# A hybrid decoder step on one core: the paged past's keys and values fetched and multiplied in alternating slots

## The chip, the cores and the metric

The program runs on 1 core of one Trainium2 chip. The engines named are PE (TensorE), DVE (VectorE), ACT (ScalarE), POOL (GpSimd, whose queue issues the page fetches) and SP (whose queue issues the other transfers). The metric is device time in microseconds of one execution; 3 runs of the kernel before are given, and one profiled execution whose trace is read.

## The reference

Two layers. Each has a half-step SwiGLU, a mixer (an SSD scan beside stick-breaking attention, one input and one output projection) and a second SwiGLU. A prompt of 16 + 512 tokens and 8 samples of 8 tokens go through together. What the change touches is the samples' attention to a past of 2048 keys, kept in pages:

```python
def sb_block(q, start, k, v, key_valid, bias):
    z = jnp.einsum('bqhd,bkhd->bhqk', q, k).astype(jnp.float32) * (SB_HEAD_DIM ** -0.5)
    z = z + bias.astype(jnp.float32)[None, :, None, None]
    ...
    log_stay = jnp.where(allowed, jax.nn.log_sigmoid(-z), 0.0)
    log_after = lax.cumsum(log_stay, axis=3, reverse=True) - log_stay
    w = jnp.where(allowed, jnp.exp(jax.nn.log_sigmoid(z) + log_after), 0.0)
    return jnp.einsum('bhqk,bkhd->bqhd', w.astype(v.dtype), v)
...
        k_past = cache_k[l][page_table].reshape(db, -1, SB_HEADS, SB_HEAD_DIM)
        v_past = cache_v[l][page_table].reshape(db, -1, SB_HEADS, SB_HEAD_DIM)
        xs, c_s, s_s, k_s, v_s = layer(xs, lp, state_conv[l], state_ssm[l], k_past, v_past, 0)
```

A weight of a key depends on all later keys of its sample (the reversed cumulative sum), so no value can be weighed before all scores of its sample are there.

## The kernel before

All 592 tokens stand as columns, 128 features to a tile. Projections and feed-forward layers are `gemm`: for each output tile, 128x296 matmuls into PSUM tiles `g`, three for each weight tile (high and low parts of both sides), by `mm3` (L605). Weights come as `raw` tiles and are split into `whi` on ACT (L595) and `wlo` on DVE (L596).

A mixer spills the residual stream, projects queries and values (`values`, L926), and then the rest of its steps are written in the order of `ORDER` (convolution, `k`, `z`, the scan in six chunks, prompt attention in 12 units, and so on), with the paged past written ahead of them all. The order in which they run is another one: a scheduler takes instructions by priority, which is the place in the program unless `ahead` moves it. `UNIT` and `PRI` hold such places, counted from the start of the past: `"ps0": 507` means that the scores of sample 0 are taken as if they stood 507 instructions behind that start. Each engine then runs its own list in that order and stops at an instruction whose inputs aren't there. So all of this is one interleaving, and `together` adds one rule: matmuls of a group stand in a row, and the first of them takes over the waits of all.

The past of a layer, in `past`: for each sample 8 key pages and 8 value pages (here a "page" is one indirect fetch of 128x1024 float32, 512 KB, on POOL's queue, L1487 and L1552). `past_scores` goes through four quarters: fetch two key pages into `kn` buffers, transpose them on DVE into two `kt` tiles (L1493), 16 matmuls into `sc`; after every second quarter sigmoids on ACT write `pbe` and `pst` (four buffers). `past_weights` makes the running product on DVE (L1298), carries it across partitions by two small transposes on PE (of `tot`, L1518, and of `car`, L1524), multiplies (L1530), transposes eight tiles (L1534) and copies them to `wt` (L1536). `past_values` goes through four quarters of two value pages, each 8 matmuls into `po`, and ends with `ob` (L1565) and two small matmuls (L1569). Key and value pages share six buffers of tag `kn`; `kt` has two, `sc` and `po` one each. The program writes the scores of sample s, then the values of sample s-1, then the weights of sample s.

The first half of the output projection `w_out` (192 matmuls of `g` from `mh`/`ml`, L605 again) needs only the scan's side. Its four parts are tied behind the last scores, weights and values; the second half needs everything, and starts behind it.

Of the kernel before, what the change touches and what calls it, by code (L numbers as in the profile page):

```python
# [8 lines left out]
F32 = mybir.dt.float32  # L9
# [75 lines left out]
def pack(d):  # L85
# [21 lines left out]
class Kern:  # L107
# [1350 lines left out]
    def past(self):  # L1458
        self.oP = self.cp.tile([128, 4, 64], F32, name="oP", tag="oP")
        todo = None  # L1460
        for s in range(8):
            with self.ahead("ps", s):
                be, st = self.past_scores(s)
            if todo:
                with self.ahead("pv", s - 1):
                    self.past_values(*todo)
            with self.ahead("pw", s):
                todo = (s, *self.past_weights(s, be, st))
        with self.ahead("pv", 7):
            self.past_values(*todo)  # L1470

    def past_scores(self, s):
        nc, l = self.nc, self.l
        qbd = self.QBD[0]
        for a in range(4):
            nc.scalar.copy(qbd[32 * a:32 * a + 32, :, a, :].rearrange("p (b m) q -> p b m q", b=4),
                                  self.rep[32 * a:32 * a + 32, :, :, 8 * s:8 * s + 8])
        be = [self.kv.tile([128, 512], F32, name="pbe", tag="pb", bufs=4) for _ in range(2)]
        st = [self.kv.tile([128, 512], F32, name="pst", tag="pb", bufs=4) for _ in range(2)]
        for half in range(2):  # L1480
            sc = self.own("sc", [128, 2, 256])
            for tb in range(2):
                kns, kts = [], []
                for u in range(2):
                    kn = self.kv.tile([128, 1024], F32, name="kn", tag="kn", bufs=6)
                    i = 4 * half + 2 * tb + u
                    nc.gpsimd.indirect_dma_start(kn, None, self.kflat,  # L1487
                                                 bass.IndirectOffsetOnAxis(ap=self.kidx[l][:, s, i:i + 1], axis=0))
                    kns.append(kn.rearrange("p (t c) -> p t c", t=2))
                for quad in range(2):  # L1490
                    kt = self.kv.tile([128, 4, 8, 32], F32, name="kt", tag="kt")
                    for u in range(2):
                        nc.vector.transpose(kt[:, 2 * u:2 * u + 2].rearrange("p t h i -> p t (h i)"),  # L1493
                                            kns[u][:, :, 256 * quad:256 * quad + 256])
                    kts.append(kt)
                with self.together():
                    for quad, dh, i in ((quad, dh, i) for quad in range(2) for dh in range(2) for i in range(4)):
                        h = 4 * quad + i
                        hd = 4 * (2 * (h % 2) + dh) + h // 2
                        self.last_sc = self.mm(sc[32 * i:32 * i + 32, quad, 128 * tb:128 * tb + 128],  # L1500
                                qbd[:, hd].rearrange("p a q -> p (a q)"), kts[quad][:, :, 2 * i + dh, :],
                                start=(dh == 0), stop=(dh == 1))
            for quad in range(2):
                c = 2 * l + quad
                f = lambda t: t.rearrange("p (i t) -> p i t", t=16)[:, :, 8 * half:8 * half + 8]
                self.sigmoids(f(be[quad]), f(st[quad]), sc[:, quad].rearrange("p (t i) -> p i t", t=8),
                              self.bq[:, c:c + 1], self.bq[:, 4 + c:5 + c])
        return be, st

    def past_weights(self, s, be, st):  # L1510
        nc = self.nc
# [15 lines left out]
        wts = []  # L1527
# [11 lines left out]
        return wts,  # L1539

    def past_values(self, s, wts):

        nc, l = self.nc, self.l
        po = self.own("po", [128, 512])
        for e in range(2):
            for a2 in range(2):
                vs = []
                for a in (2 * a2, 2 * a2 + 1):
                    tag, bufs = ("kt", 2) if s == 7 and e + a2 == 2 else ("kn", 6)
                    v = self.kv.tile([128, 2, 512], F32, name="v", tag=tag, bufs=bufs)  # L1550
                    i = s * 4 + a
                    nc.gpsimd.indirect_dma_start(v.rearrange("p k c -> p (k c)"), None, self.vflat,  # L1552
                                                 bass.IndirectOffsetOnAxis(ap=self.vidx[l][:, i, e:e + 1], axis=0))
                    vs.append((a, v))
                with self.together():
                    for a, v in vs:
                        for j in range(2):
                            for quad in range(2):
# [64 lines left out]
```

## Time and profile before

| what | value |
|---|---|
| median of 3 runs | 2719.44 us (2717.28 to 2721.03) |
| profiled execution | 2716.29 us |
| its span, first to last instruction | 2714.5 us |
| granted TensorE clock, mean | 0.983 |
| PE, DVE, ACT, POOL busy | 96%, 55%, 36%, 12% of the span |
| `g` matmuls on PE (L605) | 53% of the chain that ended last |
| key pages, value pages fetched | 128 and 128, 134 MB |

Busy times count an engine as busy while any instruction of it is in flight; matmuls overlap, so that a busy PE may still have room. A wait is put down to the semaphore that came last. A stretch is given in us from the span's start; layer 0's mixer lies between about 509 and 930 us, layer 1's between about 1854 and 2280.

### The profile page before, as it was taken

How to read it: one execution, taken by the hardware profiler on the slowest of the kernel's cores; microseconds unless marked ns; L12 is line 12 of the kernel's file. 1: busy time of each engine (PE TensorE's matmuls, PEld its weight loads, DVE VectorE, ACT ScalarE, POOL GpSimd, SP SyncE). 2: the span in 40 equal slices, each digit the busy share in tenths (PEclk: the TensorE clock that was granted, in tenths of full speed). 3: DMA queues.
4: the chain of work that ended last, by engine and by line, in shares of the span. 5: the costliest groups of instructions: out<-in, count | busy, mean ns of one | idle time of the engine just before them, and what ended most of it. 6: DMA issues, size and time to landing. Idle time of an engine off the chain costs nothing.

```text
span 2714.5 us, 51301 instructions
## 1 busy us (share of the span) xinstructions
PE 2611.9 (96%) x21547; PEld 2469.2 (91%) x21547; DVE 1505.0 (55%) x3005; ACT 981.8 (36%) x1773; POOL 315.6 (12%) x288
## 2 busy tenths in 40 slices
PE   8999999999878999999999999999997899999999
PEld 7999999888656999999999999998875579999999
DVE  5444345477886744444554343454777867434444
ACT  3323224255654332222332222233556544323222
POOL 1000000024443100000000000000334431000000
PEclk9999999999998999999999999999998989999999
DMA  3232234347776122222222323254577762222222
GB/s 111 79 116 86 79 109 130 125 142 262 269 267 230 55 78 86 86 78 78 78 78 79 101 85 94 74 157 125 183 248 247 256 219 71 78 86 86 78 87 81
DMA packets 245111, 343.28 MB, mean 126 GB/s; under 512 B 32808, under 2 KB 196720, under 8 KB 244880
## 3 DMA queue, kind: packets, MB, share of 16 engines
q1 hardware_dynamic: 208016, 205.77, 24.5%
q0 software_dynamic: 36864, 134.23, 14.5%
q8 instruction: 169, 2.77, 0.4%
q14 instruction: 62, 0.51, 0.1%
HBM read 320.29 MB, written 19.66 MB: 125 GB/s over the span
## 4 chain that ended last, share of the span: by engine, by line
PE 60%; DVE 6%; DMA 3%; ACT 2%; issue 1%; POOL 0%; SPq 0%; DVEq 0%; ACTq 0%; POOLq 0%
PE g L605 53%; DVE kt L1493 2%; DMA v<-in_cache_v,vi 1%; PE v L926 1%; DMA kn<-in_cache_k,ki 1%; PE po L208 1%; PE po L211 1%; DVE st L1298 1%; DVE x L799 0%; PE pw L476 0%; PE z L211 0%; PE sc L211 0%; DVE pst L1298 0%; PE zt L1350 0%; PE pw L1534 0%
## 5 line engine op out<-in xcount | busy, mean ns | idle before, releaser
L605 PE MATMUL g<-xl,whi 128*128 128x296 f32 (+1 forms) x3392 | 1016.9, 300 | 1.7 <-DVE xl L447 1.7
L605 PE MATMUL g<-xh,wlo 128*128 128x296 f32 (+1 forms) x3392 | 1012.5, 299 | 3.4 <-DVE wlo L596 3.4
L605 PE MATMUL g<-xh,whi 128*128 128x296 f32 (+1 forms) x3392 | 1013.8, 300 | 1.6 <-DVE gs L231 1.2
L595 ACT ACTIVATE whi<-raw 128x512 fp32r<-128x512 f32 (+1 forms) x664 | 412.7, 622 | 1363.5 <-PE g L605 1280.4
L596 DVE TENSOR_TENSOR wlo<-raw,whi 128x512 fp32r<-128x512 f32 (+1 forms) x664 | 450.7, 679 | 598.0 <-ACT whi L595 541.1
L605 PEld LDWEIGHTS g<-xh,wlo 128*128 128x128 f32 x3392 | 640.2, 189 | 5.4 <-DVE wlo L596 4.1
L605 PEld LDWEIGHTS g<-xh,whi 128*128 128x128 f32 x3392 | 639.6, 189 | 6.0 <-issue 2.6
L605 PEld LDWEIGHTS g<-xl,whi 128*128 128x128 f32 x3392 | 640.6, 189 | 4.8 <-DVE xl L447 2.8
L605 PE MATMUL g<-hl,whi 128*128 128x296 f32 (+1 forms) x1408 | 417.9, 297 | 0.0
L605 PE MATMUL g<-hh,wlo 128*128 128x296 f32 (+1 forms) x1408 | 417.7, 298 | 0.0
L605 PE MATMUL g<-hh,whi 128*128 128x296 f32 (+1 forms) x1408 | 416.8, 298 | 0.0
L1487 POOL DMA_INDIRECT kn<-in_cache_k,ki x128 | 137.0, 1070 | 1554.6 <-PE g L605 931.5
L605 PEld LDWEIGHTS g<-hl,whi 128*128 128x128 f32 x1408 | 265.2, 188 | 0.0
L605 PEld LDWEIGHTS g<-hh,wlo 128*128 128x128 f32 x1408 | 264.3, 188 | 0.0
L605 PEld LDWEIGHTS g<-hh,whi 128*128 128x128 f32 x1408 | 263.9, 188 | 0.0
L1493 DVE STREAM_TRANSPOSE kt<-kn 128x512 f32<-128x512 f32 x256 | 163.4, 680 | 41.8 <-PE sc L211 21.7
L1552 POOL DMA_INDIRECT v<-in_cache_v,vi x128 | 144.2, 1127 | 280.6 <-DVE kt L1493 128.0
L704 DVE SCALAR_TENSOR_TENSOR x<-g,x 128x296 f32<-128x296 f32 (+1 forms) x192 | 88.2, 464 | 119.1 <-PE g L605 118.5
L231 DVE TENSOR_TENSOR us<-g,R 128x296 f32<-128x296 f32 (+1 forms) x176 | 81.6, 464 | 129.5 <-PE g L605 129.4
L231 DVE TENSOR_TENSOR gs<-g,R 128x296 f32<-128x296 f32 (+1 forms) x176 | 80.7, 464 | 123.1 <-PE g L605 121.4
L691 ACT ACTIVATE hh<-us 128x592 fp32r<-128x592 f32 (+1 forms) x88 | 61.2, 696 | 62.4 <-DVE us L689 62.4
L605 PE MATMUL g<-mh,whi 128*128 128x296 f32 (+1 forms) x256 | 78.0, 305 | 2.0 <-DVE ot L231 2.0
(372 smaller groups left out, 2894.5 us busy)
## 6 DMA issues: line engine op xcount, KB each, us to landing
raw<-in_ffn_w_gu SPq DMA_DIRECT2D x176, 512.0 KB
raw<-in_ffn_w_down SPq DMA_DIRECT2D x80, 512.0 KB
raw<-in_w_in SPq DMA_DIRECT2D x44, 512.0 KB
raw<-in_w_out SPq DMA_DIRECT2D x16, 512.0 KB
spill<-x SPq DMA_DIRECT2D x16, 296.0 KB
x<-spill SPq DMA_DIRECT2D x16, 296.0 KB
raw<-in_ffn_w_down SPq DMA_DIRECT2D x16, 256.0 KB
xt<-in_x_prompt SPq DMA_DIRECT2D x8, 256.0 KB
```

What stands on the lines that cost most here:

```text
L208: i = self.nc.tensor.matmul(*a, **k).ins
L211: i = self.nc.tensor.matmul(*a, **k).ins
L231: self.nc.vector.tensor_tensor(tv[0:P, h, :], ps[h][0:P, 0:self.n], rv[0:P, h, :], ALU.mult)
L595: nc.scalar.activation(hi[:, 0:nk], s, AF.Copy)
L596: nc.vector.tensor_tensor(lo[:, 0:nk], s, hi[:, 0:nk].bitcast(F32), ALU.subtract)
L605: mm = nc.tensor.matmul(ps[h][:, 0:self.n], w[:, k, :], self.hv(x)[:, h, :], start=(first and k == 0 and i == 0), stop=(last and k == nk - ...
L691: nc.scalar.activation(hh[:, a:b], u[:, a:b], AF.Copy)
L704: nc.vector.scalar_tensor_tensor(v, p, 0.5, v, ALU.mult, ALU.add)
L926: nc.tensor.matmul(ps[c], x[:, t0:t0 + 128], w.rearrange("p x c -> p (x c)"), start=(k == 0 and i == 0), stop=(k == 7 and i == 2))
L1487: nc.gpsimd.indirect_dma_start(kn, None, self.kflat, bass.IndirectOffsetOnAxis(ap=self.kidx[l][:, s, i:i + 1], axis=0))
L1493: nc.vector.transpose(kt[:, 2 * u:2 * u + 2].rearrange("p t h i -> p t (h i)"), kns[u][:, :, 256 * quad:256 * quad + 256])
L1552: nc.gpsimd.indirect_dma_start(v.rearrange("p k c -> p (k c)"), None, self.vflat, bass.IndirectOffsetOnAxis(ap=self.vidx[l][:, i, e:e + 1] ...
```

## The change

The past is written as 34 slots and four value quarters behind them. Slot x fetches the two key pages of quarter x (four quarters to a sample) and, from slot 6, the two value pages of quarter x - 6; transposes the keys; and multiplies scores and values in one `together` group. A sample's weights are made at the end of its fourth slot, so that its values begin two slots later (slot 4s + 6). In the last two slots there are values alone, and the last sample's four value quarters follow. Operations, shapes, tags and numbers of buffers are what they were; the functions are cut anew. The 13 entries of `UNIT` for the past's units are dropped, so that the past stands at its own place in the program, ahead of all that follows; the other entries stay.

```diff
--- before.py
+++ after.py
@@ -97,8 +97,8 @@
 UNIT = {
     "conv0": 296, "conv2": 988, "conv3": 1825, "conv5": 1898, "k1": 434, "k2": 1127, "k3": 936, "prompt0": 1013,
     "prompt1": 2161, "prompt11": 2222, "prompt2": 2280, "prompt3": 1185, "prompt4": 2319, "prompt5": 1429,
-    "prompt6": 106, "prompt7": 1403, "ps0": 507, "ps3": 2030, "ps4": 1648, "ps7": 1031, "pv0": 0, "pv3": 1421,
-    "pv7": 1019, "pw0": 408, "pw3": 532, "pw4": 1425, "pw5": 0, "pw6": 2149, "pw7": 619, "scan0": 467, "scan2": 75,
+    "prompt6": 106, "prompt7": 1403,
+    "scan0": 467, "scan2": 75,
     "scan3": 879, "scan5": 123, "wo0": 0, "wo1": 2358, "wo2": 1775, "wo3": 86, "wo4": 1087, "wo5": 1599, "wo6": 529,
     "wo7": 1477, "z1": 0, "z2": 970, "z3": 1087,
 }
@@ -1456,56 +1456,78 @@
         nc.scalar.activation(self.on, po, AF.Copy)
 
     def past(self):
+
+
+        nc, l = self.nc, self.l
         self.oP = self.cp.tile([128, 4, 64], F32, name="oP", tag="oP")
-        todo = None
-        for s in range(8):
-            with self.ahead("ps", s):
-                be, st = self.past_scores(s)
-            if todo:
-                with self.ahead("pv", s - 1):
-                    self.past_values(*todo)
-            with self.ahead("pw", s):
-                todo = (s, *self.past_weights(s, be, st))
-        with self.ahead("pv", 7):
-            self.past_values(*todo)
-
...
+        wts = {}
+        late = lambda x: (x // 4, x % 4)
+        for x in range(34):
+            s, i = late(x)
+            v, vi = late(x - 6)
+            if s < 8 and i == 0:
+                qbd = self.QBD[0]
+                for a in range(4):
+                    nc.scalar.copy(qbd[32 * a:32 * a + 32, :, a, :].rearrange("p (b m) q -> p b m q", b=4),
+                                   self.rep[32 * a:32 * a + 32, :, :, 8 * s:8 * s + 8])
+                be = [self.kv.tile([128, 512], F32, name="pbe", tag="pb", bufs=4) for _ in range(2)]
+                st = [self.kv.tile([128, 512], F32, name="pst", tag="pb", bufs=4) for _ in range(2)]
+            if s < 8 and i % 2 == 0:
+                sc = self.own("sc", [128, 2, 256])
+            kns = self.key_pages(s, i) if s < 8 else None
+            vs = self.value_pages(v, vi) if v >= 0 else None
+            kts = self.turned(kns) if kns else None
+            if v >= 0 and vi == 0:
+                po = self.own("po", [128, 512])
+            with self.together():
+                if kts:
+                    self.scores(sc, i % 2, kts, qbd)
+                if vs:
+                    self.weigh(po, vi, vs, wts[v])
+            if s < 8 and i % 2:
                 for quad in range(2):
+                    c = 2 * l + quad
+                    f = lambda t: t.rearrange("p (i t) -> p i t", t=16)[:, :, 8 * (i // 2):8 * (i // 2) + 8]
+                    self.sigmoids(f(be[quad]), f(st[quad]), sc[:, quad].rearrange("p (t i) -> p i t", t=8),
+                                  self.bq[:, c:c + 1], self.bq[:, 4 + c:5 + c])
+            if v >= 0 and vi == 3:
+                self.gathered(v, po)
+            if s < 8 and i == 3:
+                wts[s] = self.past_weights(s, be, st)
+        po = self.own("po", [128, 512])
+        for vi in range(4):
+            vs = self.value_pages(7, vi)
+            with self.together():
+                self.weigh(po, vi, vs, wts[7])
+        self.gathered(7, po)
...
+    def key_pages(self, s, i):
+        kns = []
+        for u in range(2):
+            kn = self.kv.tile([128, 1024], F32, name="kn", tag="kn", bufs=6)
+            self.nc.gpsimd.indirect_dma_start(kn, None, self.kflat, bass.IndirectOffsetOnAxis(
+                ap=self.kidx[self.l][:, s, 2 * i + u:2 * i + u + 1], axis=0))
+            kns.append(kn.rearrange("p (t c) -> p t c", t=2))
+        return kns
...
+    def value_pages(self, s, i):
+        vs = []
+        e, a2 = i // 2, i % 2
+        for a in (2 * a2, 2 * a2 + 1):
+            tag, bufs = ("kt", 2) if s == 7 and i == 3 else ("kn", 6)
+            v = self.kv.tile([128, 2, 512], F32, name="v", tag=tag, bufs=bufs)
+            self.nc.gpsimd.indirect_dma_start(v.rearrange("p k c -> p (k c)"), None, self.vflat, bass.IndirectOffsetOnAxis(
+                ap=self.vidx[self.l][:, s * 4 + a, e:e + 1], axis=0))
+            vs.append((a, v))
+        return vs
+
...
```

What is left out are the bodies that moved unchanged into `turned`, `scores`, `weigh` and `gathered`, and the lines of `past_scores` and `past_values` that they replace.

What the scheduler makes of it: POOL's queue in layer 0 (`kn` are key pages, `v` value pages), the difference:

```order
-L1487 DMA kn<-in_cache_k,ki_1938 128x1024 x16
-L1552 DMA v<-in_cache_v,vi_1940 128x1024 x8
-L1487 DMA kn<-in_cache_k,ki_1938 128x1024 x8
-L1552 DMA v<-in_cache_v,vi_1940 128x1024 x8
...
-L1552 DMA v<-in_cache_v,vi_1940 128x1024 x16
+L1508 DMA kn<-in_cache_k,ki_1938 128x1024 x14
+L1569 DMA v<-in_cache_v,vi_1940 128x1024 x2
+L1508 DMA kn<-in_cache_k,ki_1938 128x1024 x2
...
+L1569 DMA v<-in_cache_v,vi_1940 128x1024 x14
```

Sixteen, then eight and eight by turns became fourteen, then two and two by turns, with fourteen value pages at the end.

PE at the start of layer 0's mixer, behind the first scores (`dtp` and `dtt` belong to the step sizes of the scan, `g` to the convolution's projection, `sc` are the scores), the difference:

```order
 L1017 MATMUL dtp_6996<-xh,dtw_1959 40x296
 L1017 MATMUL dtp_6996<-xl,dtw_1959 40x296
+L208 MATMUL sc<-kt,qbd_1946 32x128
+L211 MATMUL sc<-kt,qbd_1946 32x128 x15
 L1017 MATMUL dtp_6996<-xh,dtw_1959 40x296
 L1017 MATMUL dtp_6996<-xl,dtw_1959 40x296
+L1024 MATMUL dtt<-call,df 16x8
+L1024 MATMUL dtt<-call,df 128x8 x2
 L605 MATMUL g_7083<-xh,wlo 128x296
 L605 MATMUL g_7083<-xh,whi 128x296
```

The second quarter's scores stand among the matmuls of `dtp`; before they stood behind 158 of `g`. Counted over the whole list, 312 matmuls of `g` stood between the first scores and the first transpose of `tot`, and now 122 do; from the first to the second transpose of `tot` it was 166 `g` and 87 rows of other work (most of it the scan's), and is 264 and 30. In both lists the first `tot` stands behind five quarters' scores.

PE at the end of the past in layer 0 (`zo`, `zt` and `z` are prompt attention and its last 16 tokens, `ptn`, `pwn` and `pon` the samples' new keys, `tm` the output of `k`); before:

```order
L605 MATMUL g_9852<-mh,wlo 128x296
L208 MATMUL po<-v,wt 32x256
L211 MATMUL po<-v,wt 32x256 x7
L208 MATMUL z_9608<-wp,vk 64x16
L211 MATMUL z_9608<-wp,vk 64x16 x15
L211 MATMUL z_9608<-w_9633,vk 64x16 x4
...
L605 MATMUL g_9886<-ml,whi 128x296
L1569 MATMUL po<-call,ob 128x16 x2
```

and now:

```order
L1556 MATMUL pw<-call,pbe 128x128 x4
L1350 MATMUL zt<-call,be 128x128 x4
L208 MATMUL po<-v,wt 32x256
L211 MATMUL po<-v,wt 32x256 x7
...
L1593 MATMUL po<-call,ob 128x16 x2
L1440 MATMUL ptn<-call,tb 128x64 x4
L1447 MATMUL pwn<-call,ben 64x64 x8
L208 MATMUL zo<-wp,vk 64x128
L211 MATMUL zo<-wp,vk 64x128 x3
L897 MATMUL tm<-call,k 128x128 x12
```

Before, the last six value quarters, the last weights and the last output stood among the 192 `g` of the first half of `w_out`. Now the last sample's four value quarters stand in a row behind its weights, and the new keys, the output of `k` and all 192 `g` follow.

More of the change, by code (lines that the diff above doesn't have):

```diff
@@ L1472, in past_scores @@
[L1472 to L1489, printed above, removed]
-                for quad in range(2):
[L1491 to L1508, printed above, removed]
@@ new lines, in turned, with scores @@
+    def turned(self, kns):
+        kts = []
+        for quad in range(2):
+            kt = self.kv.tile([128, 4, 8, 32], F32, name="kt", tag="kt")
+            for u in range(2):
+                self.nc.vector.transpose(kt[:, 2 * u:2 * u + 2].rearrange("p t h i -> p t (h i)"),
+                                         kns[u][:, :, 256 * quad:256 * quad + 256])
+            kts.append(kt)
+        return kts
+    def scores(self, sc, tb, kts, qbd):
+        for quad, dh, i in ((quad, dh, i) for quad in range(2) for dh in range(2) for i in range(4)):
+            h = 4 * quad + i
+            hd = 4 * (2 * (h % 2) + dh) + h // 2
+            self.last_sc = self.mm(sc[32 * i:32 * i + 32, quad, 128 * tb:128 * tb + 128],
+                                   qbd[:, hd].rearrange("p a q -> p (a q)"), kts[quad][:, :, 2 * i + dh, :],
+                                   start=(dh == 0), stop=(dh == 1))
@@ L1538, in past_weights @@
             wts.append(wt)
[L1539 to L1558, printed above, removed]
-                                cc, g = 2 * e + j, 2 * j + quad
-                                self.last_po = self.mm(po[32 * g:32 * g + 32, 0:256],
-                                        wts[quad][:, a, 4 * cc:4 * cc + 4].rearrange("p h q -> p (h q)"),
-                                        v[:, j, 256 * quad:256 * quad + 256], start=(e == 0 and a == 0),
-                                        stop=(e == 1 and a == 3))
@@ new lines, in past_weights @@
+        return wts
+    def value_pages(self, s, i):
[8 more added lines that the diff above has]
+        return vs
@@ new lines, in weigh @@
+    def weigh(self, po, i, vs, wts):
+        e = i // 2
+        for a, v in vs:
+            for j in range(2):
+                for quad in range(2):
+                    cc, g = 2 * e + j, 2 * j + quad
+                    self.last_po = self.mm(po[32 * g:32 * g + 32, 0:256],
+                                           wts[quad][:, a, 4 * cc:4 * cc + 4].rearrange("p h q -> p (h q)"),
+                                           v[:, j, 256 * quad:256 * quad + 256], start=(e == 0 and a == 0),
+                                           stop=(e == 1 and a == 3))
@@ L1564, in past_values, with gathered @@
+    def gathered(self, s, po):
+        nc = self.nc
         ob = self.small("ob", [128, 256], bufs=1)
```

## The prediction

> **What bounds the kernel now.** I read the page's totals first, then busy time by stretch, then what each engine waited for, then the times of one recurring instruction.
>
> ```profile
> PE 2611.9 (96%) x21547; PEld 2469.2 (91%) x21547; DVE 1505.0 (55%) x3005; ACT 981.8 (36%) x1773; POOL 315.6 (12%) x288
> ```
>
> PE is busy almost throughout. Feed-forward work is at the pace of its matmuls, which a row of the chain of waits gives: 417.69 / 3058 = 0.1366 us for each matmul of `g`, though a single one lasts 0.30 us.
>
> ```profile
> 952.42 417.69 PE g L605 x3058
> ```
>
> The change touches the mixers alone. Layer 0's, cut in five (columns: stretch; its length; busy us of PE, PEld, DVE, ACT, POOL with counts; granted clock; DMA share; GB/s):
>
> ```profile
> 509.00:583.00 74.00, 74.00 (x619) 67.73 (x617) 53.86 (x133) 32.30 (x66) 11.76 (x10) 1.00 0.50 158
> 583.00:709.00 126.00, 116.08 (x1311) 98.54 (x1312) 93.36 (x215) 75.05 (x155) 46.08 (x43) 0.99 0.70 239
> 709.00:781.00 72.00, 58.49 (x746) 42.02 (x746) 62.52 (x132) 44.35 (x98) 30.78 (x30) 0.95 0.75 241
> 781.00:835.00 54.00, 40.79 (x470) 28.03 (x469) 45.16 (x103) 29.47 (x61) 24.56 (x23) 0.84 0.79 282
> 835.00:893.00 58.00, 53.89 (x599) 44.24 (x591) 33.87 (x89) 21.42 (x46) 16.20 (x15) 0.94 0.57 193
> ```
>
> First convolution, then scan and gate, then two stretches of prompt attention, then `w_out`. DVE is 87% and 84% busy in the two attention stretches, DMA about three quarters; nothing is full, so work goes round a loop of several engines. That loop is the paged past. Its beat is one instruction per sample, the transpose of `tot` on PE (layer 0's 1st, 2nd, 4th and 8th; layer 1's 1st and 8th):
>
> ```profile
> 578.80 0.27 PE L1518 MATMUL pw<-call,tot 128*128 128x128 f32 x1
> 630.48 0.27 PE L1518 MATMUL pw<-call,tot 128*128 128x128 f32 x1
> ...
> 706.61 0.33 PE L1518 MATMUL pw<-call,tot 128*128 128x128 f32 x1
> ...
> 861.17 0.27 PE L1518 MATMUL pw<-call,tot 128*128 128x128 f32 x1
> ...
> 1923.68 0.27 PE L1518 MATMUL pw<-call,tot 128*128 128x128 f32 x1
> ...
> 2213.47 0.27 PE L1518 MATMUL pw<-call,tot 128*128 128x128 f32 x1
> ```
>
> From the 2nd to the 4th a sample takes (706.61 - 630.48) / 2 = 38.1 us, from the 4th to the 8th (861.17 - 706.61) / 4 = 38.6 us. The work around it is scan and projections in the one, prompt attention in the other; the beat is the same, so the past has a pace of its own. What it waits for, from 560 to 900 us (who for whom: total, times, longest):
>
> ```profile
> POOL v L1552 <- DVE kt L1493: 69.3, 16, 17.8
> POOL v L1552 <- PE po L211: 60.2, 12, 18.6
> ...
> PE po L208 <- DMA v<-in_cache_v,vi: 15.8, 12, 3.0
> ```
>
> The queue that fetches pages stands 17 and 18 us at a time for a page buffer: eight key pages, then eight value pages, share six buffers, so fetching goes in bursts.
>
> **The change, part by part.** Pages (64 of keys and 64 of values in a layer), transposes, matmuls, activations: the same number of each. So the time can only come from order, and I sum it for layer 0 along the beat.
>
> *The start.* Ahead of the first `tot` the rows of the order show 312 `g` matmuls after the first scores before, and 122 now, the dropped entries of the table having held the past back. 190 x 0.1366 = 26.0 us earlier: 552.8. Room is there: the first stretch has DMA at 0.50 and DVE at 53.86 of 74 us. Four quarters are transposed between the first scores and that `tot`, as before, in half the time.
>
> ```profile
> L1493 DVE STREAM_TRANSPOSE kt<-kn 128x512 f32<-128x512 f32 x256 | 163.4, 680 | 41.8 <-PE sc L211 21.7 <-DMA kn<-in_cache_k,ki 15.2 <-PE px L1124 4.8
> ```
>
> 16 x 0.68 = 10.9 us on DVE, beside the 20 us that it idles there; without that cover the start would come 10.9 us later.
>
> *First to second `tot`.* 51.7 us now. The order puts 264 `g` there instead of 166 (+98, +13.4 us), and 57 fewer small scan matmuls: 0 to 7.8 us if each costs between nothing and a `g`; I take 6.0, nearer the upper, as they too follow each other through the array. 51.7 + 7.4 = 59.1, so the second `tot` comes at 611.9, 18.6 us early.
>
> *The beat.* Keys and values now alternate by two pages. Two quarters of a sample pass before its values begin, where four (a whole sample's scores) did, and one stretch of PE waits for both kinds of page. Bounds: as now at worst in this term, 38.6. From below, DVE in the two attention stretches is busy 62.52 + 45.16 = 107.7 of 126 us, and with no idleness a sample would take 38.65 x 107.7/126 = 33.0 us; DMA would by the same reckoning allow 0.77 x 38.65 = 29.8. The bursts are evened, but transposes still wait for the stretch ahead (two `kt` buffers), so I take the middle, 35.8, for four samples, 143.2 us. For the two samples under the scan, where PE is busy 116.08 of 126 us, I give only half of the waits for values back: 15.8 us over eight samples is 2.0 each, so 38.1 - 1.0 = 37.1, 74.2 us for two. The last `tot` then comes at 611.9 + 74.2 + 143.2 = 829.3 instead of 861.17.
>
> *The end.* Here the change loses. From the last `tot` to the last sample's output 25.7 us pass, and I keep that: the weights' chain (transposes, DVE products, a copy) is the same and the last value quarters follow it as now.
>
> ```profile
> 854.18 0.40 PE L605 MATMUL g<-mh,whi 128*128 128x296 f32 x1
> ...
> 886.85 0.42 DVE L1565 TENSOR_TENSOR ob<-po,call 128x256 f32<-128x256 f32 x1 [3.78 <-PE po L211]
> ...
> 899.06 0.30 PE L605 MATMUL g<-mh,wlo 128*128 128x296 f32 x1
> ```
>
> But now the first 192 matmuls of `w_out` run from 854.18 to 899.06 and hide the last six value quarters and the last weights. In the new order all 192 stand behind the last output. The same stretch without them:
>
> ```profile
> L211 PE MATMUL po<-v,wt 128*32 128x256 f32 x84 | 7.7, 467 | 0.0
> L208 PE MATMUL po<-v,wt 128*32 128x256 f32 x12 | 4.6, 470 | 1.0 <-DMA v<-in_cache_v,vi 1.0
> ...
> L1534 PE MATMUL pw<-call,pbe 128*128 128x128 f32 x8 | 1.3, 281 | 0.0
> ```
>
> ```profile
> 2194.35 1.97 PE L897 MATMUL tm<-call,k 128*128 128x128 f32 x8
> 2196.11 1.02 PE L1534 MATMUL pw<-call,pbe 128*128 128x128 f32 x4
> ...
> 2199.83 0.35 PE L1447 MATMUL pwn<-call,ben 64*64 64x64 f32 x3
> ```
>
> 44.9 - 7.7 (values) - 1.0 (a wait) - 1.3 (weights), plus the key output's and new keys' transposes, which moved behind the past (2194.35 to 2200.18 in layer 1, less the weights' 1.02 between them: 4.8), is 39.7. It can't be under 192 x 0.1366 = 26.2, nor need it exceed 44.9 by much. So `w_out`'s first half ends at 829.3 + 25.7 + 39.7 = 894.7 instead of 899.1: 4.4 us a layer. Layer 1's beat is (2213.47 - 1923.68) / 7 = 41.4 against 40.3 us, near enough to take the same: 8.8 us in all.
>
> The profiled execution took 2716.3 us, of which 2714.5 is the span; 1.8 lies around it and stays. The median of the runs, 2719.4, is 3.1 above it. 2719.4 - 8.8 = 2710.6; I say **2711**.
>
> The waits for pages also let the granted clock sink: 1.00 in the first stretch, 0.84 in the fourth. On this the Trainium skill ("TensorE: Matmul & The Clock Gate", Part 1) says that an idle window of some 3.4 us halves the clock and that sustained work restores it. Longest single wait for a value page here: 3.0 us, close to that and with a mean clock that has sunk, so the trace fits the rule; it speaks against the change, since one stretch that waits for both pages idles longer at once. By it the sum would be worse by the 7.7 us a layer that the slower case below works out from rows, 2726.
>
> On the pages' own time:
>
> ```profile
> kn<-in_cache_k,ki POOLq DMA_INDIRECT x128, 6.4
> ```
>
> 6.4 us from issue to landing. The Trainium skill's "DMA: Bandwidth & Descriptors" (Anatomy of one DMA, the gpsimd path) gives a fit of 2.0 us plus bytes over 436 GB/s, which for 512 KB is an estimate of 3.2. The trace has twice that, with several pages in flight, and decides; by the fit no page would be late and the sum would be the case of 2684 below.
>
> **The rivals.** The break-even matters most: the end stays at 899.1 if the six samples from 611.9 take 221.8 us, 37.0 each. I forecast 36.2; today it is 38.4. One microsecond a sample decides the sign, and about 5 us of the whole (0.2%) is what a measurement of this kernel can tell from no change.
>
> - *The loop evens out fully* (chance 0.24). Four samples at DVE's 33.0, two at 38.1 - 2.0: 611.9 + 72.2 + 132.0 + 25.7 + 39.7 = 881.5, 17.6 a layer better: 35 us, **2684**. For it: no engine is full. Against: the 25.7 us from the last `tot` to its output show how long the chain inside a sample is.
> - *The past keeps its pace* (0.22). 38.4 each: 611.9 + 230.7 + 65.4 = 908.0, 8.9 a layer worse, **2737**. For it: the beat was the same beside two different kinds of work. Against: bursts with 18 us stops are gone.
> - *One stretch waits for the later page* (0.12, slower). Place: the 26 stretches a layer that hold both. Price: each waits the present mean, 15.8 / 12 = 1.3 us, 34 instead of 15.8: +18 on the last case, 27 a layer, **2773**; if the clock of the fourth stretch held in the third too, PE's 58.49 us there became 66.2 (x 0.95/0.84), 7.7 more. From 4.4 / 26 = 0.17 us a stretch above my sum, the gain is gone. Against: two pages lead, as before.
> - *Hidden anyway* (0.05). The prompt's attention sets the end of its stretches, the past only fills: **2719**.
>
> **How the numbers follow.** My forecast has 0.37; its beat may be 35.5 to 37.4, 2702 to 2724, of which 0.23 is faster by over 0.2% and 0.14 within. With the rivals: faster 0.23 + 0.24 = 0.47; same 0.14 + 0.05 = 0.19; slower 0.22 + 0.12 = 0.34. The range for 8 in 10 takes in the evened loop and the unchanged pace with the end's bound (44.9 instead of 39.7, both layers, +10): 2680 to 2752. Around the forecast alone: 2700 to 2725.
>
> **What would show it.** The first `tot` near 553 us, the second near 612: right on the start. `tot` 35 to 36 us apart afterwards, and no stop of the page queue over 10 us: right on the beat; 38 or more: wrong, and slower. `w_out`'s first half unbroken, some 40 us behind the last output: right on the end. Waits of `sc` or `po` for `v` above 16 us in a mixer, or a clock below 0.84 in the attention stretches: the fourth case. What would break it whole is a conv that stalls because its splits queue behind transposes on DVE.

## The result, and the profile after

The change takes 2685.0 us (median of 4 runs, 2681.4 to 2688.4), the kernel before 2718.4 beside it: a ratio of 0.988 (95% interval 0.9865 to 0.9894), 33 us faster. A second comparison, on the chip of the last four experiments, gave 0.989 (0.987 to 0.991). The forecast was 2711, 8.8 us faster, and its rival "the loop evens out fully" had 2684.

First the page's totals after; PE is busy 11.4 us less (2611.9 before), with the same 21547 matmuls.

```profile
PE 2600.5 (97%) x21547; PEld 2466.6 (92%) x21547; DVE 1505.1 (56%) x3005; ACT 978.9 (37%) x1771; POOL 304.7 (11%) x288
```

Next the first, second, third, sixth, seventh and eighth transpose of `tot` in layer 0, then layer 1's first and eighth (start us, length, engine, line).

```profile
550.98 0.27 PE L1540 MATMUL pw<-call,tot 128*128 128x128 f32 x1
599.41 0.27 PE L1540 MATMUL pw<-call,tot 128*128 128x128 f32 x1
635.83 0.33 PE L1540 MATMUL pw<-call,tot 128*128 128x128 f32 x1
...
733.04 0.27 PE L1540 MATMUL pw<-call,tot 128*128 128x128 f32 x1
783.66 0.33 PE L1540 MATMUL pw<-call,tot 128*128 128x128 f32 x1
818.82 0.33 PE L1540 MATMUL pw<-call,tot 128*128 128x128 f32 x1
...
1877.31 0.27 PE L1540 MATMUL pw<-call,tot 128*128 128x128 f32 x1
...
2150.12 0.28 PE L1540 MATMUL pw<-call,tot 128*128 128x128 f32 x1
```

The last one comes 42 us earlier than before. From the third to the sixth a sample takes (733.04 - 635.83) / 3 = 32.4 us, then one takes 50.6. In that stretch PE's list holds prompt attention and the samples' scan states, and the page queue stands 16.6 us in it for matmuls that come late. The queue has four stops of over 10 us between 560 and 900 us (17.1, 13.0, 16.6 and 17.0). Its waits there (total, times, longest), and below them one of PE's:

```profile
POOL kn L1508 <- PE po L211: 91.0, 23, 17.1
POOL v L1569 <- PE po L211: 17.9, 4, 17.0
...
PE sc L208 <- DMA v<-in_cache_v,vi: 4.8, 6, 1.6
```

The last line is the shared stretch waiting for a value page: 4.8 us, and 1.5 more stand at `po`, where it was 15.8 before. The fourth case's mark (over 16 us) isn't there, nor is its clock: 0.85 and 0.96 in the two attention stretches (the columns are those of the prediction's stretches), whose DVE is 85% and 87% busy.

```profile
716.00:784.00 68.00, 60.03 (x750) 44.17 (x743) 57.48 (x123) 35.32 (x82) 30.82 (x30) 0.85 0.77 247
784.00:823.00 39.00, 32.72 (x333) 21.77 (x332) 33.84 (x81) 24.17 (x48) 16.22 (x15) 0.96 0.69 239
```

The end of layer 0's mixer: last value quarters, last matmuls of prompt attention (`zo`), `k`'s output (`tm`), then the first and last of `w_out`'s first half.

```profile
839.04 0.41 DVE L1589 TENSOR_TENSOR ob<-po,call 128x256 f32<-128x256 f32 x1
...
841.69 0.49 PE L211 MATMUL zo<-wp,vk 128*64 128x128 f32 x5
842.11 1.53 PE L897 MATMUL tm<-call,k 128*128 128x128 f32 x12
...
846.69 0.41 PE L605 MATMUL g<-mh,whi 128*128 128x296 f32 x1
...
882.11 0.30 PE L605 MATMUL g<-mh,wlo 128*128 128x296 f32 x1
```

Before, prompt attention ended at about the same time:

```profile
839.73 0.49 PE L211 MATMUL zo<-wp,vk 128*64 128x128 f32 x5
```

The reading that carries the rest is the two mixers as wholes, from the first work on the samples' queries to the last matmul of `w_out`. Columns: stretch; its length; busy us of PE, PEld, DVE, ACT, POOL with counts; granted clock; DMA share; GB/s. Before:

```profile
509.00:930.00 421.00, 379.40 (x3996) 316.22 (x3994) 316.54 (x719) 218.19 (x452) 135.24 (x123) 0.96 0.62 209
1854.00:2279.00 425.00, 383.93 (x3995) 317.33 (x3993) 313.68 (x715) 223.62 (x454) 141.43 (x123) 0.94 0.62 207
```

and after:

```profile
508.00:912.00 404.00, 375.83 (x3996) 316.31 (x3995) 316.88 (x715) 219.75 (x453) 133.51 (x124) 0.96 0.64 217
1835.00:2243.00 408.00, 376.27 (x3990) 314.61 (x3989) 315.11 (x712) 218.79 (x450) 134.66 (x123) 0.95 0.63 215
```

Both together went from 846 to 812 us; outside them nothing changed (2714.5 - 846 = 1868.5 us of the span before, 2679.6 - 812 = 1867.6 after). Of the 34 us, 22.8 are PE's waits (length less busy time: 82.7 before, 59.9 after), and 11.2 are busy time, with the same matmuls. The second follows the clock in part: length x (1 - clock) is 42.3 us before and 36.6 after, by two-digit clocks.

### The profile page after: what moved, and what is told of

It is laid out like the page before. It is cut to its first block, busy times and chain, and to the rows that moved or that the text cites. A ratio compares the mean times of both kernels' runs of the same rounds, so it can differ in the third digit from the quotient of the medians.

```text
span 2679.6 us, 51326 instructions
## 1 busy us (share of the span) xinstructions
PE 2600.5 (97%) x21547; PEld 2466.6 (92%) x21547; DVE 1505.1 (56%) x3005; ACT 978.9 (37%) x1771; POOL 304.7 (11%) x288
## 4 chain that ended last, share of the span: by engine, by line
PE 84%; DVE 7%; issue 3%; ACT 3%; DMA 2%; POOL 1%; SPq 0%; DVEq 0%; POOLq 0%; ACTq 0%
PE g L605 72%; PE v L926 2%; DVE kt L1519 2%; PE po L211 1%; PE sc L211 1%; DMA v<-in_cache_v,vi 1%; DVE st L1298 1%; PE pw L476 1%; DMA kn<-in_cache_k,ki 1%; DVE pst L1298 1%; POOL v L1569 0%; PE z L208 0%; PE z L211 0%; DVE xl L447 0%; DVE wlo L596 0%
## 5 line engine op out<-in xcount | busy, mean ns | idle before, releaser
L1508 POOL DMA_INDIRECT kn<-in_cache_k,ki x128 | 128.3, 1003 | 1657.9 <-PE g L605 934.8
L1519 DVE STREAM_TRANSPOSE kt<-kn 128x512 f32<-128x512 f32 x256 | 162.9, 681 | 27.7 <-PE sc L211 14.5
```

The costliest lines, as they stand in the source:

```text
L1508: self.nc.gpsimd.indirect_dma_start(kn, None, self.kflat, bass.IndirectOffsetOnAxis(ap=self.kidx[self.l][:, s, 2 * i + u:2 * i + u + 1], a ...
L1519: self.nc.vector.transpose(kt[:, 2 * u:2 * u + 2].rearrange("p t h i -> p t (h i)"), kns[u][:, :, 256 * quad:256 * quad + 256])
```

## The experiments

Three theories at the start. A, mine: alternating pages even the loop of the paged past. B: the earlier start, from the dropped entries, is the gain. D: the shared stretch of PE is the gain. Two more came on the way. Ratios are to the kernel before on the same chip. The second four ran on a chip where the kernel before took 2764.3 us; their traces are compared among themselves alone.

| run | ratio, 95% interval |
|---|---|
| only the entries dropped | 1.0011 (0.9998 to 1.0025) |
| scores and values in two groups | 0.9951 (0.993 to 0.9972) |
| past held back at the start | 0.9915 (0.9898 to 0.9931) |
| pages four and four | 0.9977 (0.9963 to 0.9991) |
| values one slot late | 0.9906 (0.9874 to 0.9937) |
| five page buffers | 0.9909 (0.9893 to 0.9926) |
| two groups, values fetched first | 0.9974 (0.996 to 0.9987) |
| sample states first, `w_out` untied | 0.9883 (0.9867 to 0.99) |
| the change again | 0.9889 (0.9869 to 0.9909) |
| pages one and one | 0.9959 (0.9939 to 0.998) |
| before, no value pages | 1.0058 (1.0037 to 1.008) |
| the change, no value pages | 0.9926 (0.9903 to 0.995) |

**Only the entries dropped.** The kernel before, with `UNIT` shortened as in the change:

```diff
-    "prompt6": 106, "prompt7": 1403, "ps0": 507, "ps3": 2030, ... "pw6": 2149, "pw7": 619, "scan0": 467, "scan2": 75,
+    "prompt6": 106, "prompt7": 1403, "scan0": 467, "scan2": 75,
```

> The kernel before with only the 13 entries of UNIT for the past's units dropped: pages still come eight keys, eight values, and scores and values stay in stretches of their own. Its PE order has the same 122 matmuls of g ahead of the first transpose of tot as the change. Theory A (alternating pages shorten the beat; the start is the smaller part): first tot near 551 us, as in the change, but then a beat as before, about 38 us, so the last tot of layer 0 near 599 + 6 x 38.4 = 830 us instead of 818.8; 2700 to 2710 us. Rival B (the whole gain is the earlier start that the dropped entries give): 2685 us, within 5 of the change. Rival C (the entries were worth their place): 2719 or slower.

No gain, so B falls, and A's 2700 to 2710 too; the time is C's. Its first `tot` is at 551.2 and its last at 827.3, nearly as in the change, and yet it ends where the kernel before does. Its mixers, and the end of layer 0's:

```profile
507.00:940.00 433.00, 389.41 (x3997) 320.16 (x3997) 317.55 (x721) 222.56 (x456) 135.81 (x123) 0.93 0.61 203
1864.00:2288.00 424.00, 387.76 (x3995) 317.85 (x3995) 315.10 (x717) 216.64 (x451) 138.42 (x123) 0.94 0.62 207
```

```profile
844.76 0.42 DVE L1564 TENSOR_TENSOR ob<-po,call 128x256 f32<-128x256 f32 x1 [1.59 <-PE po L210]
```

```profile
860.79 0.85 PE L210 MATMUL zo<-wp,vk 128*64 128x128 f32 x5
...
869.68 0.38 PE L604 MATMUL g<-mh,whi 128*128 128x296 f32 x1
```

The past is done at 844.8, but prompt attention only at 861.6, where it ended at 840.2 before (839.73 + 0.49) and 842.2 in the change. What the past won, prompt attention lost, and the second half of `w_out` needs both.

**Scores and values in two groups.**

```diff
-            with self.together():
-                if kts:
-                    self.scores(sc, i % 2, kts, qbd)
-                if vs:
-                    self.weigh(po, vi, vs, wts[v])
+            if kts:
+                with self.together():
+                    self.scores(sc, i % 2, kts, qbd)
+            if vs:
+                with self.together():
+                    self.weigh(po, vi, vs, wts[v])
```

> The change, but scores and values of a slot in two groups of their own, so that PE can run one when the other's pages are late; pages still alternate by two. Theory A (the gain is in the order of the pages): 2685 us within 5, beat 36 to 37. Rival D (the gain is in the shared stretch of PE): half of the gain or more is lost, 2700 us or more. The other side of D, my fourth case of the prediction (a shared stretch waits for the later page): 2680 or less.

Over half of the gain goes, as D expected, so the change needs the shared stretch, though it isn't the whole gain. Value pages are waited for on PE twice as long and more, layer 0's line and layer 1's:

```profile
PE po L208 <- DMA v<-in_cache_v,vi: 13.7, 8, 3.1
...
PE po L208 <- DMA v<-in_cache_v,vi: 14.0, 7, 4.6
```

27.7 us, against 4.8 + 1.5 + 2.1 + 1.8 = 10.2 in the change. That made a theory F: the values' lateness hides behind the keys' transposes. It is tested below.

**Past held back at the start.** The change, with slots 0 to 5 taken as if they stood 800 instructions later:

```diff
         for x in range(34):
+            with self.ahead("ps", x):
...
+    **{f"ps{x}": 800 for x in range(6)},
```

> The change, but its first six slots held back in priority, so that 311 matmuls of g stand ahead of the first transpose of tot, as before the change (312), instead of 122; everything else as in the change. Theory A with a start that counts in full: first tot near 577 us, all later ones 26 us late, 2685 + 2 x 26 = 2737. Theory A with the start hidden (the mixer is set by how full PE is kept, not by when the past begins): under 2700 us, later gaps of tot shorter than in the change. Rival B (the gain is the start): 2719 or more.

The first `tot` came at 578.6, 27.6 us late, and the last output of layer 0 at 868.1, 29 us late; the time lost only 7 to 10 us in both layers together (0.9915 against 0.9879 and 0.9889). So the start is mostly hidden. Later gaps of `tot` were not shorter, as that branch of the expectation had them: `w_out`'s first half, whose first `g` stands at 851.3, covered the past's end again.

**Pages four and four, and one and one.** Only the order of the fetches in the program changes:

```diff
-            kns = self.key_pages(s, i) if s < 8 else None
-            vs = self.value_pages(v, vi) if v >= 0 else None
+            if x % 2 == 0:
+                kq = [self.key_pages(s, i + d) if s < 8 else None for d in range(2)]
+                vq = [self.value_pages(v, vi + d) if v >= 0 else None for d in range(2)]
+            kns, vs = kq[x % 2], vq[x % 2]
```

> The change, but pages fetched four keys, four values by turns instead of two and two; the groups on PE as in the change. Theory A: between the two, waits of the page queue longer than 17 us come back and the beat grows by about 0.5 to 1 us a sample: 2690 to 2700 us. Rivals B and D, for which the order of pages counts for nothing: 2685 us within 4.

> The change, but inside a slot the pages alternate one by one (key, value, key, value) instead of two and two; the groups on PE as in the change. Theory A (finer alternation keeps buffers coming free evenly: eight by eight gave 1.001 of the kernel before, four by four 0.998, two by two 0.988): at or below the change, 0.985 to 0.988. Rival (the two keys of a quarter are needed together, first, and their transposes on DVE start later when a value page lies between them): 0.990 to 0.995.

Both lose more than A gave them: four and four about four fifths of the gain, one and one about two thirds (its rival's side). A finer alternation is not better as such. But the fetches are not the only thing that moves: the scheduler puts the engines' lists together around them. One and one tells the two apart for a while: in layer 0 PE, DVE and ACT work in the same order as in the change (but for neighbours that swap) up to the fourth `tot`, and this stands 167.2 us behind the mixer's start, where the change has 161.0 and its repetition 162.3. So about 5 us can be put down to the fetches; the other 16 or so of the 22 us that this mixer is longer (426 and 404) come later, where the lists differ. For four and four, whose lists differ from 85 us on, the runs can't say whether it is the pages or the lists. PE waits no longer for pages in four and four than in the change (8.6 us in both layers, 10.2 there); it is slow in layer 0, with a clock that sank:

```profile
508.00:937.00 429.00, 390.72 (x3992) 324.34 (x3991) 317.50 (x716) 216.34 (x449) 133.74 (x123) 0.92 0.61 205
1859.00:2269.00 410.00, 376.09 (x3990) 314.56 (x3989) 313.96 (x710) 224.10 (x455) 141.56 (x123) 0.95 0.64 214
```

**Values one slot late.** `late(x - 6)` becomes `late(x - 5)`, the loop one slot shorter.

> The change, but values one slot late instead of two (slot 4s + 5 instead of 4s + 6). In the change the last scores of a sample are followed by its weights after 30.1, 24.5 and 23.1 us (587.0 to 617.1, 625.9 to 650.4, 660.1 to 683.2), and its first values start 2.4 to 3.2 us behind the weights. Theory E (this chain of weights paces the loop: three slots of a sample lie inside the chain and one outside): with one slot less inside it, a sample takes about one slot of 7.5 us more, beat 41 to 44; PE can fill only part of it, 2720 us or more. Theory A alone (the order of the pages is what counts): beat 36 to 37, 2685 us within 6.

The beat grew as theory E says, to (853.70 - 599.48) / 6 = 42.4 us in layer 0 and 45.6 in layer 1, but the time did not follow: 0.9906, 5 to 7 us over the change, where E had 35 or more.

```profile
599.48 0.33 PE L1540 MATMUL pw<-call,tot 128*128 128x128 f32 x1
...
853.70 0.33 PE L1540 MATMUL pw<-call,tot 128*128 128x128 f32 x1 [1.94 <-DVE tot L1537]
...
1953.46 0.33 PE L1540 MATMUL pw<-call,tot 128*128 128x128 f32 x1
...
2227.11 0.27 PE L1540 MATMUL pw<-call,tot 128*128 128x128 f32 x1
```

The run of five buffers, on the same chip, has 38.9 us in both layers and the same time. So E is right on the beat and wrong on the time, and the beat is not what the time is made of.

**Five page buffers.** `bufs=6` of tag `kn` becomes 5 everywhere.

> The change with five page buffers instead of six, nothing else. A slot holds four pages. Theory A with the buffers as the loop's limit (a page is fetched when one comes free, and the page queue stands 91 us for PE in layer 0): a sixth of the pages in flight is gone, beat longer by 1.5 us or more, waits of PE for pages from 10 us in both mixers to 20 or more, 2700 us or more. Theory E (the weights' chain sets the loop, pages have room): 2685 us within 5.

0.9909, 5 to 8 us over the change, between both theories; layer 0's mixer starts at 514 us instead of 508 (the tag serves the loading of the tokens too), so that most of this can lie ahead of the past. The beat, 38.9 us, is 2.3 longer than in the change on the other chip, as A had it, and PE waits 14.3 us for value pages in both mixers; the time hardly follows. A sixth buffer is not what the gain rests on.

**Two groups, values fetched first.** The run with two groups, and

```diff
-            kns = self.key_pages(s, i) if s < 8 else None
             vs = self.value_pages(v, vi) if v >= 0 else None
+            kns = self.key_pages(s, i) if s < 8 else None
```

> The change with scores and values of a slot in two groups of their own (as in the run with groups apart, 2704 us) and, in each slot, the two value pages fetched ahead of the two key pages. In the run with groups apart PE waits 27.7 us for value pages in both mixers, in the change 10.2. Theory F (the shared stretch gains because the value pages arrive while the key pages are still transposed, so that their lateness costs nothing): with values fetched first PE's waits for value pages fall to 12 us or less, and the time comes back to 2685 to 2695 us. Rival (the gain of the shared stretch lies elsewhere, as in the times at which buffers come free): waits of PE for pages may fall, but the time stays at 2700 us or more.

PE's waits for value pages are 14.1 us (6.5 and 7.6) where 27.7 stood, on another chip, and the time got worse, 0.9974. But as much stands now inside the scores' matmuls, 14.1 us in both layers, where the run with two groups has none; the profile shows nothing that PE waits for there ("issue"). Layer 0's lines, then layer 1's:

```profile
PE sc L211 <- issue: 7.3, 14, 1.0
PE po L208 <- DMA v<-in_cache_v,vi: 6.5, 3, 2.4
...
PE po L208 <- DMA v<-in_cache_v,vi: 7.6, 2, 4.5
PE sc L211 <- issue: 6.8, 10, 1.1
```

So the waits moved rather than went, and this run doesn't settle F: it shows only that fetching values first did not bring the time back.

**Sample states first, `w_out` untied.**

```diff
-        for c, (t0, L) in enumerate(CHUNKS):
+        for c in (5, 0, 1, 2, 3, 4):
+            t0, L = CHUNKS[c]
...
-                      after=(self.last_sc, self.last_sc, self.last_pw, self.last_po)[mp])
+                      after=None)
```

> The change with three things more: the scan's chunk of the samples (with their 8 states) is written ahead of the prompt's five chunks instead of behind them, mix takes the place of the past's start in PRI, and w_out's first half is no longer tied behind the last scores, weights and values. Meant to be faster: in the change the states' steps lie between 733 and 786 us, in the stretches where PE waits most, and the 50.7 us from the sixth to the seventh tot hold them. Theory E/A: the stop goes (no gap of tot over 43 us in layer 0), 2665 to 2680 us. Rival (the mixer is set by its DVE and ACT work in the attention, whatever stands where): 2685 us within 5, with the waits moved to an earlier stretch.

Meant to be faster than the change, it is the same (0.9883). The stop moved: gaps of 45 and 50 us stand one and two samples earlier. The rival had this.

**The change again.**

> The change itself, unaltered, on the chip of this call, so that the three runs beside it have their comparison there. All theories: 0.986 to 0.990 of the kernel before.

As expected; 2689.5 us on this chip, 30.7 below the kernel before.

**No value pages,** in the kernel before and in the change: 64 of a layer's 128 fetches left out, the matmuls kept.

```diff
-                    v = self.kv.tile([128, 2, 512], F32, name="v", tag=tag, bufs=bufs)
-                    nc.gpsimd.indirect_dma_start(v.rearrange("p k c -> p (k c)"), None, self.vflat, ...)
+                    v = self.vfix
```

> The kernel before, with no value page fetched: the values' matmuls read one fixed tile (filled once), so that the outputs of the samples' attention are not the reference's; key pages have five buffers of their own. All operations on PE, DVE and ACT stay. Theory A (what separates the two kernels is how PE waits for pages and how the page buffers go round): without values both kernels lose that part, this one comes to within 8 us of the change without values, 0.975 to 0.985 of the kernel before. Rival (the pages are not it; PE's order and the earlier start are): this one stays within 10 us of the kernel before and 20 us or more above the change without values.

> The change, with no value page fetched, in the same way (fixed tile; key pages have five buffers; outputs of the samples' attention not the reference's). Theory A: a little below the change, 0.975 to 0.985 of the kernel before, within 8 us of the kernel before without values. Rival: 20 us or more below the kernel before without values.

Here A falls. Without value pages the kernel before takes 2736.9 us and the change 2699.7: neither became faster (2720.1 and 2689.5 with them on this chip), and the difference is still 37 us. (Both start layer 0's mixer 6 to 7 us later, at 515, for the fifth buffer as above.) The mixers of the one and of the other:

```profile
515.00:944.00 429.00, 386.98 (x3995) 323.67 (x3993) 317.03 (x716) 224.52 (x456) 71.37 (x60) 0.92 0.41 128
1870.00:2298.00 428.00, 389.78 (x3990) 324.11 (x3989) 315.86 (x713) 221.37 (x451) 76.90 (x60) 0.91 0.41 128
```

```profile
515.00:922.00 407.00, 379.21 (x3994) 318.73 (x3993) 313.73 (x716) 222.91 (x456) 68.66 (x61) 0.95 0.42 135
1844.00:2262.00 418.00, 384.82 (x3992) 321.96 (x3991) 314.38 (x710) 219.23 (x451) 64.30 (x60) 0.93 0.41 131
```

And the second and eighth `tot` of the change without values:

```profile
605.42 0.27 PE L1542 MATMUL pw<-call,tot 128*128 128x128 f32 x1
...
823.93 0.33 PE L1542 MATMUL pw<-call,tot 128*128 128x128 f32 x1 [0.53 <-DVE tot L1539]
```

DMA share 0.42 instead of 0.64, and the same beat, (823.93 - 605.42) / 6 = 36.4 us (36.6 with values). In the kernel before, the 41.6 us that PE waits in layer 0 with value pages are 42.0 without them: other waits took the place of those for pages, each small (its first three groups below). Leaving the pages out moved the lists too: in layer 0 PE keeps the order that it has with value pages (but for neighbours that swap) for the first 58 us of the mixer in the kernel before and 129 in the change. So each of the two is a new interleaving, and what they show is that the 37 us between the kernels don't need the value pages' fetching.

```profile
PE pS L1120 <- ACT dec L1113: 3.4, 1, 3.4
PE sc L208 <- ACT pst L1295: 3.4, 3, 1.7
PE zo L208 <- ACT wp L1354: 3.0, 4, 1.3
```

**All runs of one kind of chip side by side.** Both mixers together, from the sums of such rows, and for each layer the us from the mixer's start at which the past's last output and the last `zo` of prompt attention stand:

| kernel | length | PE busy | PE waits | last output of the past | last `zo` |
|---|---|---|---|---|---|
| before | 846 | 763.3 | 82.7 | 381, 387 | 331, 340 |
| change | 812 | 752.1 | 59.9 | 332, 336 | 334, 333 |
| change again | 821 | 757.9 | 63.1 | 333, 343 | 335, 340 |
| entries dropped | 857 | 777.2 | 79.8 | 340, 353 | 354, 354 |
| two groups | 832 | 755.0 | 77.0 | 347, 343 | 349, 345 |
| held back | 828 | 755.8 | 72.2 | 362, 357 | 336, 332 |
| four and four | 839 | 766.8 | 72.2 | 340, 344 | 351, 333 |
| one and one | 839 | 759.3 | 79.7 | 336, 345 | 351, 344 |
| before, no values | 857 | 776.8 | 80.3 | 379, 379 | 351, 350 |
| change, no values | 825 | 764.0 | 61.0 | 326, 334 | 332, 344 |

Two streams share PE, DVE and ACT: the past and prompt attention. `w_out` closes the mixer, its second half behind both. Before, the past ended 47 to 50 us behind prompt attention; in the change they end within 3 us of each other, with prompt attention 3 us later in one layer than before and 7 earlier in the other. The two executions of the change differ by 9 us in length and 3.2 in waits, and in layer 1 by 7 us at both ends, so a single difference of that size says nothing. What is clear of it: in layer 0 the four other orders with an early past (entries dropped, two groups, four and four, one and one) have the past's end 3 to 15 us later than the change, and prompt attention ends 14 to 20 us later than in either execution of it; in layer 1 only the run with the entries dropped does so (354, against 333 and 340). And PE's waits are near 60 us only in the change and in the change without value pages, 72 to 83 in the rest of the table.

What stays open is why. The runs show that the earlier start alone brings nothing (entries dropped), that most of the gain is lost without the shared stretch or without the two-by-two order, and that the two kernels differ as much with no value page fetched. From this I argue that the gain lies in the order of the work on the engines and not in the value pages' transfers; it isn't shown by itself, since any edit of the past moves the lists of PE, DVE and ACT together, and key pages were fetched in every run. Which place in the lists makes prompt attention wait less was not found.

## Why the prediction was right or wrong

The sign and the range held; the forecast was 26 us too slow, and its gain, 8.8 us, about a quarter of the 33 measured. By its own steps, in layer 0:

- *The start*, 552.8: measured 551.0, right, and the cover on DVE held. But its worth was less than its 26 us a layer: holding it back cost 7 to 10 us in both.
- *First to second `tot`*, 59.1: measured 48.4. This is the largest mis-sized term, 10.7 us. I had priced "57 fewer small scan matmuls" at 6.0 and bounded them at a `g` each, 7.8. But 57 were rows of the order, and a row can hold many matmuls: beside `g`, PE has 324 matmuls in this stretch before and 216 after, 108 fewer, which at a `g` each is 14.8. With 98 `g` more the stretch became 3.3 us shorter, so that what left it was worth 51.7 + 13.4 - 48.4 = 16.7. PE's idle time in it went from 5.6 to 1.6, and its busy time rose by 0.7 with 13.4 of `g` added (rows below): 4.0 of the 16.7 were waits, 12.7 busy time, the matmuls themselves and the clock that they ran at (0.97). In layer 1 the same stretch became longer, 54.7 where 52.0 stood.
- *The beat*, 217.4 us for six samples: measured 219.4 (218.1 in layer 1). Right as a sum, not in its parts: 36.4 and 33.1 under the scan (37.1 forecast), then 31.6 and 32.5, one stop of 50.6, and 35.2 (35.8 each). The mark "no stop of the page queue over 10 us" failed: there are four, up to 17.1.
- *The end*: last `tot` to output 25.7 forecast, 20.2 measured (17.7 in layer 1), mis-sized by 5.5; `w_out`'s first half 39.7 behind the output forecast, 43.1 and 40.1 measured, unbroken as said. It ends at 882.1, not 894.7, 17.0 us ahead of 899.1 where I had 4.4.
- *Layer 1 alike*: right as a sum, 17 us in each mixer.
- *The clock*: by the rule of idle windows the sum would have been worse. It was better, and the shared stretch waited less for values than the stretches before it. "The waits for pages also let the granted clock sink" isn't borne out either: with no value page to wait for, the kernel before has 0.92 and 0.91 in its mixers, where it has 0.96 and 0.94 with them.
- *The rival of 2684* matches the time by luck. It had six samples in 204.2 us and DVE as their floor; they took 219.4, and what it missed there the other terms made up.

The stretch from the first to the second `tot`, before and after (columns as above; the counts take in what is in flight at the edges):

```profile
578.80:630.50 51.70, 46.14 (x494) 40.11 (x493) 33.62 (x75) 27.66 (x58) 20.39 (x16) 0.97 0.62 204
551.00:599.40 48.40, 46.80 (x483) 43.68 (x481) 46.45 (x111) 26.50 (x61) 18.90 (x16) 1.00 0.67 206
```

Deeper, the frame failed where it called the past's beat the path: "The beat is the same, so the past has a pace of its own", and the page buffers' bursts as what sets that pace. Without value pages the beat stays, 36.4; with one slot less of lag it is 42.4 and more, where five buffers have 38.9 on the same chip at the same time. The break-even of 37.0 us a sample, from which one microsecond decided the sign, was a property of that frame: the run with two groups has (837.8 - 603.4) / 6 = 39.1 and is faster than before, and the one with the entries dropped (827.3 - 603.6) / 6 = 37.3 and isn't. My rival "hidden anyway", in which prompt attention sets the end, had 0.05; in layer 0 of the change it ends last, by 2 us, in layer 1 the past by 3, so that a further gain in the past alone may be hidden in this way (that wasn't tried).

On the pages, the Trainium skill's fit ("DMA: Bandwidth & Descriptors", Anatomy of one DMA) would have led to 2684, close to what came. The trace doesn't bear that reason out: key pages take 5.7 us and value pages 6.6 from issue to landing in the change, not the 3.2 estimated from the fit, and the runs without value pages show that the value pages' time doesn't decide.

## What to carry to other kernels

Where an engine is nine tenths busy, as PE is here, a loop's beat inside the stretch needn't be the path: judge a new order by that engine's waits and its granted clock over the whole stretch, and see which of the streams that share it ends last. A wait that stands first in the list of waits may only be covering others; leave its cause out once (here, no value pages at all) before reckoning with it, and look whether the lists moved with it. Where a scheduler makes the lists, an edit of one stream is an edit of all: a part of a change that gains nothing alone (the dropped entries) may still be part of what gains. And count instructions, not rows of a list, before pricing them.

## What the runs showed of the hardware

In the change the granted clock falls to one half for 3.4 us or a few times that, without PE standing still so long. 3.4 us at a time (the same columns as above):

```profile
713.23:716.64 3.41, 2.44 (x45) 1.97 (x47) 3.38 (x14) 2.44 (x4) 1.68 (x2) 1.00 0.84 262
716.64:720.05 3.41, 3.41 (x43) 1.84 (x37) 3.12 (x9) 0.34 (x2) 1.90 (x3) 0.50 0.84 261
...
740.54:743.95 3.41, 1.33 (x13) 1.14 (x12) 3.41 (x7) 2.86 (x7) 2.80 (x3) 1.00 0.99 349
743.95:747.36 3.41, 3.22 (x20) 2.52 (x20) 3.41 (x9) 1.58 (x3) 0.13 (x1) 0.50 0.95 344
...
856.60:860.00 3.40, 3.40 (x47) 3.34 (x47) 0.22 (x1) 0.03 (x1) 0.00 (x0) 1.00 0.00 0
860.00:863.40 3.40, 3.40 (x16) 3.35 (x14) 1.55 (x3) 0.60 (x1) 0.00 (x0) 0.50 0.27 67
```

Half clock followed steps in which PE was 72% and 39% busy, in small pieces, and once a step with PE busy throughout, most of whose 47 matmuls are small ones of `z`, 16 columns each. The matmuls bear it out: those of `g` start 0.14 us apart just ahead of 860 us, and 0.25 apart behind it. The Trainium skill ("TensorE: Matmul & The Clock Gate", Part 1), in its table of the two states, has the half clock follow an idle window of about 3.4 us. The length of the steps agrees; an idle window isn't there: PE's longest wait between 700 and 765 us is 2.2 us. What triggers it can't be told from these runs. Each step at half clock costs 1.7 us of full-speed work, and length x (1 - clock) is between 29 and 73 us in the kernels of the last table, where PE's waits are 60 to 83: the clock is a term of the sum that can't be left out.
